# Stage 1 of layer 0 by single k tiles, 1/rms broadcast from a column, and some low parts of weights made by an adding DMA

## The chip, the cores and the metric

The kernel runs on one core of a Trainium2 chip. The metric is the device time of one execution in microseconds (us). Each kernel is run several times; the median counts. A profiled execution gives the trace that the views below are taken from. TensorE is called PE, VectorE DVE, ScalarE ACT, GpSimd POOL and SyncE SP.

## The reference

Two layers of a mixer over 256 latent tokens and 256 context tokens of 2048 features. Cut to what matters here:

```python
for l in range(2):
    shift, scale, gate = split(silu(c) @ w_mod[l] + b_mod[l], 3)   # and the same of c_ctx for the context
    h = rmsnorm(x, g_pre[l]) * (1 + scale) + shift                 # and h_c of ctx
    proj = h @ w_in[l]                                             # 5120 columns: a_u a_v a_g q k v b_g c_x c_g
    y_a = gelu(a_u) * (w_sgu @ rmsnorm(gelu(a_v)) + b_sgu) * silu(a_g)
    y_b = windowed_attention(q, k, v, k_ctx, v_ctx, sink) * silu(b_g)
    y_c = (real(fft2(c_x)) @ w_fourier + b_fourier) * silu(c_g)
    y = rmsnorm(concat(y_a, y_b, y_c) @ w_out[l], g_post[l])
    x = x + gate * y                                               # and ctx in layer 0
```

All is float32. The output is x of the latents after layer 1.

## The kernel before, in words

**Products.** Activations lie feature-major: 16 k tiles of 128 features by 512 tokens (latents, then context). A float32 product is made of three float32r products, `mm3` (L383 to L386): every operand is split into a high part (a cast by ACT) and a low part (the difference, by DVE), and high x high, high x low and low x high are added in PSUM.

**Weights.** The class `Stream` (L329 to L379) hands out `w_in` and `w_out` in halves of 128 x 1024 (512 KB). `emit` loads one into one of three `raw` tiles, lets ACT cast it (`whi`, L367) and DVE subtract (`wlo`, L368); there are four tiles of each. `next` hands out the next half and first emits as many as `NEAR` or `AHEAD = 3` says, so a half is begun when PE comes to the one three before. `pace` then lets a few steps of the other modulation columns follow on DVE (`mod_dve`, L196 to L218).

**Order.** PE's instructions are in the order of the program (`manual_schedule`, L989); the other engines are ordered by the planner, which goes by priority. Work that comes back to PE after other engines had their part stands in generators of the class `Later`; a number given with `yield` is the PE time that shall pass before the next part.

**Start and stage 1 of layer 0.** `ct`, `vecs` and the first constants are loaded, then the 16 tiles of x (L997); ACT squares them and DVE adds the squares (L464 to L468). `col_sums` sums over features on PE, `rstd_cols` (L410) makes 1/rms in a column per 128 tokens with a power on POOL, `rstd_diag` (L417) multiplies the identity by each column on DVE, and `bcast` (L431) multiplies ones by these diagonals, so that 1/rms stands on all partitions. Scale and shift of layer 0 come from PE: `mod_start(k0, nk)` (L154 to L194) loads the columns of `w_mod` of one or two k tiles in four groups of four rows of blocks, each 1 MB for a pair and 512 KB for a single k tile, multiplies them by silu(c) in four column groups of the array (L172), transposes the result on DVE (L177), and adds the four quadrants by four small products (`ps_modc`, L182). Then DVE and ACT make h of the k tile (`make_h`, L445). The first eight k tiles go as pairs, the last eight singly (`PAIRS`, `ALONE`, L24). For each block the loop of `layer` (L524) makes h, does the modulation products of the next block around its own products, and adds to four PSUM tiles of a_v and two of a_u (`start_av`, `start_au`), with k outermost. The heads 2 and 3 of a_u are units of their own behind it (`tunit`, L473, 48 products each).

**PSUM** has eight banks: six `mm` and two `ms` (small results: modulation, sums, broadcasts, transposes).

**Behind stage 1.** Branch A (L580 to L603) applies Gelu on ACT to a_u and a_v, squares, normalises, and multiplies by `w_sgu` on PE (`ps_mix`, L596) 12 units of PE time later; the Fourier branch, gates and attention follow, then the output projection, whose `boundary` (L908) makes x of layer 1 and its 1/rms by the same diagonals.

Of the kernel before, what the change touches and what calls it, by code (L numbers as in the profile page):

```python
# [23 lines left out]
PAIRS, ALONE = [0, 2, 4, 6], list(range(8, KT))  # L24
# [3 lines left out]
def units():  # L28
    """(name, first column, columns, first k tile, k tiles): blocks of w_in of 128 x 2048 each."""
    u = []  # L30
    u += [("av", COL["av"], 512, 4 * i, 4) for i in range(4)]
    u += [("au01", COL["au"], 256, 8 * i, 8) for i in range(2)]
    u += [(f"au{h}", COL["au"] + 128 * h, 128, 0, 16) for h in (2, 3)]
    u += [(f"cx{h}", COL["cx"] + 128 * h, 128, 0, 16) for h in range(4)]
    u += [(f"ag{h}", COL["ag"] + 128 * h, 128, 0, 16) for h in range(4)]
    u += [(f"cg{h}", COL["cg"] + 128 * h, 128, 0, 16) for h in range(4)]
    u += [(f"k{h}", COL["k"] + 128 * h, 128, 0, 16) for h in range(2)]
    u += [("v", COL["v"], 256, 8 * i, 8) for i in range(2)]
    u += [(f"q{h}", COL["q"] + 128 * h, 128, 0, 16) for h in range(8)]
    u += [(f"bg{h}", COL["bg"] + 128 * h, 128, 0, 16) for h in range(8)]  # L40
    return u
# [25 lines left out]
def trunk_kernel(ctx: ExitStack, tc: tile.TileContext, xT, xhalf, cT, wss, wsl, wmod, win, wout0, wout1, const, vec, rows,  # L67
# [24 lines left out]
    # ---- constants  # L92
    ct = sb([P, KT, 2], F32, "ct")
    DMA.dma_start(ct, cT)
    vecs = sb([P, 2, NVEC], F32, "vecs")
    DMA.dma_start(vecs, vec)
# [8 lines left out]
    A.activation(cs, ct, AF.Silu)  # L105
    cpad = sb([P, KT, 32], F32, "kt0")
    V.memset(cpad, 0.0)
    V.tensor_copy(cpad[:, :, 0:2], cs)

    class low:  # L110
        """instructions that may wait for the next `n`."""
# [22 lines left out]
    # ---- modulation: columns [128, 16, stream] of scale, shift and gate  # L134
# [5 lines left out]
    def mod_cols(l, cb, ps8):  # L140
        """ps8 [128, 4, 2]: silu(c) @ w_mod for 512 columns of column block cb."""
        what, j0 = cb // 4, (cb % 4) * 4
        b = vc(l, "bmod")[:, cb * 4:cb * 4 + 4].unsqueeze(2).to_broadcast([P, 4, 2])
        sl = slice(j0, j0 + 4)
        if what == 0:
            V.tensor_tensor(out=sh[l][:, sl], in0=ps8, in1=b, op=ALU.add)
        else:
            dst = (gs[l] if what == 1 else gg0)[:, sl]
            g = vc(l, "gpre" if what == 1 else "gpost")[:, sl].unsqueeze(2).to_broadcast([P, 4, 2])
            V.scalar_tensor_tensor(out=dst, in0=ps8, scalar=1.0 if what == 1 else 0.0, in1=b,  # L150
                                   op0=ALU.add, op1=ALU.add)
            V.tensor_tensor(out=dst, in0=dst, in1=g, op=ALU.mult)

    def mod_start(k0, nk):  # L154
        """scale and shift of k tiles k0 .. k0 + nk - 1 of layer 0 on the tensor engine: yields after
        each unit's products, and before the columns."""
        ps = ms_ps("mod")
        n = 2 * P * nk
        for kg in range(4):
            src = wss[PAIRS.index(k0), kg] if nk == 2 else wsl[ALONE.index(k0), kg]  # L160
            if nk == 1:
                tags = (("mraw", "mraw", "macc", "vv"), ("mg", "mgl", "yo0 yo1", "yo2 yo3"))[k0 % 2][kg]
# [33 lines left out]
    def mod_dve(l, cb, red):  # L196
        """red [128, 2, 16]: sums over the 32 partitions of each quadrant, transposed."""
# [38 lines left out]
    def mod_gate1():  # L236
        """products of silu(c) and the gate's columns of w_mod in layer 1, still to be summed over partitions."""
# [16 lines left out]
    def gate1():  # L254
        """(sum + b_mod) * g_post of layer 1's gate, on all partitions."""
# [23 lines left out]
    NEAR = [1] * 6 + [0] * 6 + [1, 2, 3]  # L279
    LOWC = 60  # L280
    YT = 2.0
# [5 lines left out]
    def pace():  # L287
        """steps of the modulation due per half of a unit, behind the latest weights on the vector engine."""
# [6 lines left out]
    # ---- work of other engines that hands products back to the tensor engine later  # L295
    class Later:
# [19 lines left out]
        def flush(self):  # L316
# [8 lines left out]
            (("yo8 yo9", 1), ("yo10 yo11", 1)), (("yo12 yo13", 1), ("yo14 yo15", 1))]  # L325
    BACK = 8

    # ---- weights: raw -> exact parts hi + lo, in halves of a unit, ahead of their use
    class Stream:  # L329
        AHEAD = 3  # L330

        def __init__(self):
            self.src, self.out, self.pos, self.stop = [], [], 0, 0
            self.place, self.behind = {}, {}
            for l in range(2):
                def half(name, i, h):
                    return win[l, UIDX[name][i], h]
                for i in range(2):
                    self.src += [half("av", 2 * i, 0), half("au01", i, 0), half("av", 2 * i, 1),
                                 half("av", 2 * i + 1, 0), half("au01", i, 1), half("av", 2 * i + 1, 1)]  # L340
                for i, u in enumerate(UNITS):
                    if u[0] not in ("av", "au01"):
# [5 lines left out]
                if l == 0:  # L348
                    n = len(self.src) - 2 * HELD
                    self.place[n] = (("mraw", 2), ("mraw", 2))  # L350
                    self.place[n + 1] = (("macc", 1), ("mg", 1))
            for i, tags in enumerate(TAIL):
                self.place[len(self.src) - len(TAIL) + i] = tags

        def emit(self):
            tags = self.place.get(len(self.out), (("whi", NHI), ("wlo", NLO)))
            r = sb([P, 1024], F32, "raw", NRAW)
            DMA.dma_start(r, self.src[len(self.out)])
            hi, lo = ([sb([P, 1024 // len(t[0].split())], F32R, tag, t[1]) for tag in t[0].split()] for t in tags)
            with ExitStack() as after:  # L360
# [27 lines left out]
    def part(w, c):  # L388
        """columns c of both parts; a part is a tile or a list of tiles side by side."""
# [19 lines left out]
    # ---- per-token reciprocal rms from sums over features  # L409
# [7 lines left out]
    def rstd_diag(sums, n, dim):  # L417
        r = rstd_cols(sums, n, dim)
        dg = w2k([P, n, P])
        for j in range(n):  # L420
            V.tensor_scalar(out=dg[:, j], in0=ident, scalar1=r[:, j:j + 1], scalar2=None, op0=ALU.mult)
# [9 lines left out]
    def bcast(dg, n):  # L431
        ps = ms_ps("rb")
        PE.matmul(ps[:, 0:n * P], ones, dg.rearrange("p a b -> p (a b)"), start=True, stop=True)
        return ps

    # ---- streams in feature-major tiles
    yo = [None] * KT
# [7 lines left out]
    def make_h(l, k, rb, streams):  # L445
        """h = x * rstd * gs + sh, as hi + lo; rb: rstd over the tokens of `streams`."""
# [26 lines left out]
    def tunit(n, sl=None):  # L473
        """feature-major product of one unit of 128 columns: PSUM [128, n]."""
# [18 lines left out]
    blocks = [(k, 2) for k in PAIRS] + [(k, 1) for k in ALONE]  # L493

    # ---- one layer, up to the inputs of the output projection
    def layer(l):
# [12 lines left out]
        # a_v (token-major) and two heads of a_u, k outermost  # L509
        av = [mm_ps("av") for _ in range(nt)]  # L510
        au = [mm_ps("au") for _ in range(2)]
# [12 lines left out]
        for i, (k0, nk) in enumerate(blocks):  # L524
            mod = mod_start(*blocks[i + 1]) if l == 0 and i + 1 < len(blocks) else iter(())

            def step():
                next(mod, None)

            for k in range(k0, k0 + nk):  # L530
                made = prep_h(l, k)
            if l == 1 and i == 0:
# [7 lines left out]
            for _ in range(2 if nk == 2 else 4):  # L540
                step()
            start_av(k0, range(nt))
            if nk == 2:
                start_au(k0)
                step()
                step()
                start_av(k0 + 1, range(nt // 2))
            step()
            if nk == 2:
                start_av(k0 + 1, range(nt // 2, nt))  # L550
# [28 lines left out]
        # branch A  # L579
        def branch_a():  # L580
            vt = [w2k([P, 512]) for _ in range(nt)]
            ss = sb([P, 4], F32, "ss")
            for j in range(2):
# [8 lines left out]
            yield 12.0 if l == 0 else 7.0  # L592
            for h in range(4):
# [9 lines left out]
                yield (12.0 if h == 1 else 2.0) if l == 0 else (7.0 if h == 1 else 2.0)  # L603

        # branch C
# [137 lines left out]
        for h in (2, 3):  # L743
# [56 lines left out]
    # ---- output projection  # L800
# [107 lines left out]
    def boundary(s, acc):  # L908
        """x1 = x0 + gate * y / rms(y) of stream s in place, and its own 1 / rms."""
# [11 lines left out]
        dg = rstd_diag(ps[:, 0:2], 2, D)  # L921
# [31 lines left out]
        dg = rstd_diag(ps[:, 0:2], 2, D)  # L953
# [5 lines left out]

    def prep_h(l, k):  # L960
        new_h(k)
        if l == 0:
            return make_h(0, k, rb0, [0, 1])
        return make_h(1, k, rbs[0], [0])
# [24 lines left out]
    with tc.manual_schedule(engines={mybir.EngineType.PE}):  # L989
# [3 lines left out]
        A.copy(identr, raw[:, 0:P])  # L993
        A.copy(cst[:, 0:NFIRST - P], raw[:, P:])
        for k in range(KT):
            yo[k] = sb([P, T], F32, f"yo{k}")
            DMA.dma_start(yo[k], xT[k])  # L997
# [3 lines left out]
        m = mod_start(*blocks[0])  # L1001
# [8 lines left out]
        next(m)  # L1010
        W.emit()
        W.emit()
        list(m)
# [81 lines left out]
```

## Time and profile before

| | us |
|---|---|
| median of 3 runs | 1170.88 (1170.09 to 1171.65) |
| span of the profiled execution | 1167.9 |
| PE waits for its first operand | 17.0 |
| first product of a_v starts | 37.3 |
| last product of a_u's first two heads starts | 136.4 |
| POOL busy in all | 17.3 |

The profiled execution's own time is its span, from the first to the last instruction; what lies around it in a timed run is not in the profile. In the timeline a row has start, duration, engine, line, operation, output and inputs and the number merged; a float32 product has two records. The durations of PE overlap, since products are pipelined: the distance of two starts tells what one costs, not its duration. In the stretches the columns are busy time of each engine with its number of instructions, the granted clock of PE (1.00 is full), the share of the DMA engines and GB/s.

### The profile page before, as it was taken

What the parts mean: (1) busy time and instruction counts of PE and PEld (TensorE: products, weight loads), DVE (VectorE), ACT (ScalarE), POOL (GpSimd) and SP (SyncE); (2) the same over time, 40 slices, a digit from 0 to 9 for tenths busy, and PEclk for the clock granted to TensorE, in tenths of its full rate; (3) what the DMA queues carried; (4) which work ended last, traced back from release to release, by engine and by line L of the source; (5) the groups of instructions that cost most, each with busy time, mean ns of one, the idle gap of its engine ahead of it and who ended that gap; (6) DMA issues with size and microseconds to landing.
All of it is one profiled execution on the core that took longest, in us unless ns stands there. A gap on an engine that the chain in (4) does not pass through costs nothing.

```text
span 1167.9 us, 17483 instructions
## 1 busy us (share of the span) xinstructions
PE 1136.0 (97%) x6656; PEld 953.7 (82%) x6656; DVE 881.8 (76%) x1469; ACT 509.8 (44%) x914; POOL 17.3 (1%) x23
## 2 busy tenths in 40 slices
PE   3999999999999999999999999999999999999996
PEld 1466688888898888888888888889899999997885
DVE  5454498888988878798989886495896678888554
ACT  4222513322224667632533233365563278745442
POOL 0000000000000000000000000200000000000001
PEclk9999999999999999999999999999999999999998
DMA  9999765466665334455466665365656665688563
GB/s 339 378 387 357 254 196 166 145 202 193 200 200 178 105 114 136 134 175 173 158 199 209 205 216 162 109 207 173 205 158 205 203 200 178 195 269 244 190 187 120
DMA packets 73892, 234.32 MB, mean 201 GB/s; under 512 B 8528, under 2 KB 9680, under 8 KB 73808
## 3 DMA queue, kind: packets, MB, share of 16 engines
q1 hardware_dynamic: 73808, 233.21, 61.6%
q8 instruction: 52, 0.85, 0.3%
q14 instruction: 32, 0.26, 0.1%
HBM read 231.08 MB, written 2.10 MB: 200 GB/s over the span
## 4 chain that ended last, share of the span: by engine, by line
PE 92%; DVE 3%; DMA 2%; ACT 2%; issue 1%; POOL 0%; SPq 0%; DVEq 0%; ACTq 0%; POOLq 0%
PE ps_t L384 20%; PE ps_t L385 20%; PE ps_t L386 20%; PE ps_mod L172 3%; PE ps_av L384 2%; PE ps_y L386 2%; PE ps_y L384 2%; PE ps_y L385 2%; PE ps_av L385 2%; PE ps_av L386 2%; PE ps_v L386 1%; PE ps_v L384 1%; PE ps_v L385 1%; PE ps_tp L722 1%; PE ps_au L384 1%
## 5 line engine op out<-in xcount | busy, mean ns | idle before, releaser
L384 PE MATMUL ps_t<-hh,whi 128*128 128x512 f32 (+1 forms) x1296 | 452.1, 349 | 0.0
L386 PE MATMUL ps_t<-hh,wlo 128*128 128x512 f32 (+1 forms) x1296 | 447.4, 345 | 0.0
L385 PE MATMUL ps_t<-hl,whi 128*128 128x512 f32 (+1 forms) x1296 | 447.0, 345 | 0.0
L367 ACT CAST whi<-raw 128x1024 fp32r<-128x1024 f32 x218 | 228.2, 1050 | 397.3 <-PE ps_t L385 274.4
L368 DVE TENSOR_TENSOR wlo<-raw,whi 128x1024 fp32r<-128x1024 f32 x218 | 265.3, 1220 | 99.1 <-ACT whi L367 98.8
L384 PEld LDWEIGHTS ps_t<-hh,whi 128*128 128x128 f32 x1296 | 244.9, 189 | 34.3 <-issue 4.6
L386 PEld LDWEIGHTS ps_t<-hh,wlo 128*128 128x128 f32 x1296 | 244.7, 189 | 30.6
L385 PEld LDWEIGHTS ps_t<-hl,whi 128*128 128x128 f32 x1296 | 244.9, 189 | 28.9 <-issue 0.5
L209 DVE SCALAR_TENSOR_TENSOR macc<-mraw,cs,macc 128x512 f32<-128x512 f32 x360 | 249.9, 745 | 17.6 <-DMA mraw<-in_wmod_dram 17.5
L455 ACT ACTIVATE hh<-w2k,sh 128x256 fp32r<-128x256 f32 x64 | 29.0, 502 | 61.4 <-DVE w2k L451 61.4
L384 PE MATMUL ps_y<-whi,hh 128*128 128x512 f32 x112 | 45.0, 401 | 0.0
L386 PE MATMUL ps_y<-whi,hl 128*128 128x512 f32 x112 | 43.8, 392 | 0.0
L385 PE MATMUL ps_y<-wlo,hh 128*128 128x512 f32 x112 | 43.7, 390 | 0.0
L384 PE MATMUL ps_av<-whi,hh 128*128 128x512 f32 x96 | 40.0, 416 | 0.0
L385 PE MATMUL ps_av<-wlo,hh 128*128 128x512 f32 x96 | 37.9, 395 | 0.4 <-DVE wlo L368 0.4
L172 PE MATMUL ps_mod<-hh,kt 128*32 128x512 f32 x64 | 21.5, 649 | 17.0 <-DMA hh<-in_wss_dram 17.0
L386 PE MATMUL ps_av<-whi,hl 128*128 128x512 f32 x96 | 37.6, 392 | 0.0
L386 PE MATMUL ps_v<-whi,hl 128*128 128x256 f32 x128 | 36.2, 283 | 0.0
L384 PE MATMUL ps_v<-whi,hh 128*128 128x256 f32 x128 | 36.2, 283 | 0.0
L385 PE MATMUL ps_v<-wlo,hh 128*128 128x256 f32 x128 | 36.2, 283 | 0.0
L468 DVE TENSOR_TENSOR acc<-acc,w2k 128x512 f32<-128x512 f32 (+1 forms) x33 | 21.2, 641 | 18.7 <-ACT w2k L467 17.2
L401 ACT CAST w2k<-ps_tp 128x512 fp32r<-128x512 f32 x40 | 23.5, 587 | 22.8 <-PE ps_scc L385 12.0
(292 smaller groups left out, 1491.8 us busy)
## 6 DMA issues: line engine op xcount, KB each, us to landing
raw<-in_win_dram SPq DMA_DIRECT2D x160, 512.0 KB, 4.1
mraw<-in_wmod_dram SPq DMA_DIRECT2D x128, 512.0 KB, 4.3
raw<-in_wout_dram SPq DMA_DIRECT2D x64, 512.0 KB, 4.2
hh<-in_wss_dram SPq DMA_DIRECT2D x32, 256.0 KB, 5.6
hl<-in_wss_dram SPq DMA_DIRECT2D x32, 256.0 KB, 5.4
yo<-in_xT_dram SPq DMA_DIRECT2D x16, 256.0 KB, 5.4
mraw<-in_wsl_dram SPq DMA_DIRECT2D x8, 512.0 KB, 6.9
yo<-in_wsl_dram SPq DMA_DIRECT2D x16, 256.0 KB, 7.2
```

The lines of the kernel that those rows point to most:

```text
L172: PE.matmul(ps[32 * kk:32 * kk + 32, 0:n], cpad[:, kg * 4 + kk], ws[kk], start=kg == 0, stop=kg == 3, tile_position=(0, 32 * kk))
L209: V.scalar_tensor_tensor(out=acc[:, s], in0=w[:, kk % 2], scalar=c, in1=acc[:, s], op0=ALU.mult, op1=ALU.add)
L367: A.copy(ph, r[:, c])
L368: self.last = V.tensor_tensor(out=pl, in0=r[:, c], in1=ph.bitcast(F32), op=ALU.subtract)
L384: PE.matmul(ps, st[0], mv[0], start=start, stop=False)
L385: PE.matmul(ps, st[0], mv[1], start=False, stop=False)
L386: PE.matmul(ps, st[1], mv[0], start=False, stop=stop)
L401: A.copy(hi, src)
L455: first = A.activation(hh[k][:, sl], t[:, sl], AF.Identity, bias=sh[l][:, k, s:s + 1])
L468: V.tensor_tensor(out=acc[:, sl], in0=acc[:, sl], in1=q[:, sl], op=ALU.add)
L722: PE.transpose(tp[:, (2 * j + b) * P:(2 * j + b + 1) * P], src, ident)
```

## The change

- Layer 0's stage 1 goes by single k tiles throughout. Ahead of a_v of k tile k all products of the modulation of k + 1 stand. A third head of a_u is added in the same loop, in one of the two `ms` banks; its unit behind the loop goes. Two steps of other modulation are put at each of the last two k tiles.
- DVE, ACT and SP are ordered by hand too until the last k tile but one; `LOADS` and `SPLITS` say at which k tile a half of weights is loaded and split. x is loaded ahead of the constants and `vecs`.
- 48 products of ones by ones stand on PE ahead of the first modulation.
- `bcast` takes the column of 1/rms itself, spread over 128 columns, as the stationary operand and the identity as the moving one; `rstd_diag` goes, also in the boundaries.
- In layer 0, every other half of weights from the 22nd on (42 halves) gets its low part otherwise: ACT writes the negated high part, and a DMA issued by POOL adds the raw weights to it.
- Branch A's delays are 9 and 4 instead of 12 and 12 in layer 0.

```diff
-PAIRS, ALONE = [0, 2, 4, 6], list(range(8, KT))
+PAIRS, ALONE = [0], list(range(KT))
...
-    NEAR = [1] * 6 + [0] * 6 + [1, 2, 3]
+    NEAR = [0] * 14 + [1, 2, 3]
+    LOADS = [0, 1, 2, 4, 5, 6, 6, 8, 9, 10, 12, 13, 14]
+    SPLITS = [1, 2, 3, 5, 6, 7, 7, 9, 10, 11, 13, 14, 15]
+    WARM = 48
+    AU2 = [(("hh12 hl12", 1), ("hh13 hl13", 1)), (("yo4 yo5", 1), ("yo6 yo7", 1))]
...
+                    self.by_dma |= set(range(22, n, 2))
...
+            if tags == (("whi", NHI), ("wlo", NLO)) and len(self.out) in self.by_dma:
+                A.copy(hi[0], r)
+                A.activation(lo[0], hi[0].bitcast(F32), AF.Copy, scale=-1.0)
+                G.dma_start(lo[0], r, accum_op=ALU.add)
+                self.out.append((hi, lo))
+                return
...
-    def rstd_diag(sums, n, dim):
-        r = rstd_cols(sums, n, dim)
-        dg = w2k([P, n, P])
-        for j in range(n):
-            V.tensor_scalar(out=dg[:, j], in0=ident, scalar1=r[:, j:j + 1], scalar2=None, op0=ALU.mult)
-        return dg
-    def bcast(dg, n):
+    def bcast(r, n):
         ps = ms_ps("rb")
-        PE.matmul(ps[:, 0:n * P], ones, dg.rearrange("p a b -> p (a b)"), start=True, stop=True)
+        for j in range(n):
+            PE.matmul(ps[:, j * P:(j + 1) * P], r[:, j:j + 1].to_broadcast([P, P]), ident, start=True, stop=True)
         return ps
...
+        au = [mm_ps("au") for _ in range(2)] + [ms_ps("au") for _ in range(1 - l)]
...
+            if l == 0:
+                mm3(au[2], part(au2w, slice((k % 8) * P, (k % 8 + 1) * P)), (hh[k], hl[k]), k == 0, k == KT - 1)
...
+        if l == 0:
+            for k in range(KT):
+                new_h(k)
+                make_h(0, k, rb0, [0, 1])
+                m = mod_start(k + 1, 1) if k + 1 < KT else iter([None] * 4)
+                for _ in range(4):
+                    next(m)
+                for _ in range(LOADS.count(k)):
+                    W.load()
+                for _ in range(SPLITS.count(k)):
+                    W.emit()
...
+                start_av(k, range(nt))
+                list(m)
+                if k == KT - 2:
+                    first_stage.close()
...
+                start_au(k)
...
-            yield 12.0 if l == 0 else 7.0
+            yield 9.0 if l == 0 else 7.0
...
+        first_stage.enter_context(tc.manual_schedule(engines={EN.DVE, EN.Activation, EN.SP}))
+        DMA.dma_start(ct, cT)
+        for k in range(KT):
+            DMA.dma_start(yo[k], xT[k])
...
+        W.load()
+        ps = ms_ps("ones")
+        for _ in range(WARM):
+            PE.matmul(ps[:, 0:P], ones, ones, start=True, stop=True)
+        m = mod_start(0, 1)
+        next(m)
         ps = ms_ps("rs")
         col_sums(ps, acc0, 4)
-        dg = rstd_diag(ps[:, 0:4], 4, D)
+        r0 = rstd_cols(ps[:, 0:4], 4, D)
+        W.emit()
         next(m)
-        rb = bcast(dg, 4)
+        next(m)
+        next(m)
+        rb = bcast(r0, 4)
         rb0 = w2k([P, T])
         V.tensor_copy(rb0, rb)
+        W.load()
+        W.load()
+        list(m)
         W.emit()
         W.emit()
-        list(m)
         layer(0)
```

More of the change, by code (lines that the diff above doesn't have):

```diff
@@ L90, in ms_ps @@
         return psum.tile([P, 512], F32, tag="ms", bufs=2, name=f"ps_{name}_{cnt[0]}")
+    yo = [sb([P, T], F32, f"yo{k}") for k in range(KT)]
     ct = sb([P, KT, 2], F32, "ct")
-    DMA.dma_start(ct, cT)
     vecs = sb([P, 2, NVEC], F32, "vecs")
-    DMA.dma_start(vecs, vec)
     cst = sb([P, NKEEP - P], F32, "cst")
@@ L161, in mod_start @@
             if nk == 1:
-                tags = (("mraw", "mraw", "macc", "vv"), ("mg", "mgl", "yo0 yo1", "yo2 yo3"))[k0 % 2][kg]
+                odd = ("hh14 hl14", "hh15 hl15") if k0 < 8 else ("yo0 yo1", "yo2 yo3")
+                tags = (("mraw", "mraw", "macc", "vv"), ("mg", "mgl") + odd)[k0 % 2][kg]
             else:
@@ L333, in __init__ @@
             self.src, self.out, self.pos, self.stop = [], [], 0, 0
-            self.place, self.behind = {}, {}
+            self.raws = []
+            self.place, self.behind, self.by_dma = {}, {}, set()
             for l in range(2):
@@ L338, in __init__ @@
                 for i in range(2):
-                    self.src += [half("av", 2 * i, 0), half("au01", i, 0), half("av", 2 * i, 1),
+                    third = [half("au2", 0, i)] if l == 0 else []
+                    if l == 0:
+                        self.place[len(self.src) + 2] = AU2[i]
+                    self.src += [half("av", 2 * i, 0), half("au01", i, 0), *third, half("av", 2 * i, 1),
                                  half("av", 2 * i + 1, 0), half("au01", i, 1), half("av", 2 * i + 1, 1)]
                 for i, u in enumerate(UNITS):
-                    if u[0] not in ("av", "au01"):
+                    if u[0] not in ("av", "au01") + ("au2",) * (l == 0):
                         self.src += [win[l, i, 0], win[l, i, 1]]
@@ L491, in hold_unit @@
         return ps
-    blocks = [(k, 2) for k in PAIRS] + [(k, 1) for k in ALONE]
+    blocks = [(k, 2) for k in range(0, 8, 2)] + [(k, 1) for k in range(8, KT)]
     def layer(l):
@@ L521, in start_au @@
                 mm3(au[j][:, 0:n], part(auw, c), (hh[k][:, 0:n], hl[k][:, 0:n]), k == 0, k == KT - 1)
+            if l == 0:
+                mm3(au[2], part(au2w, slice((k % 8) * P, (k % 8 + 1) * P)), (hh[k], hl[k]), k == 0, k == KT - 1)
             later.tick(PASS * 512 * nt + PASS * n * 2)
[L524 to L528, printed above, removed]
+        if l == 0:
+            for k in range(KT):
[8 more added lines that the diff above has]
+                    W.emit()
+                if k % 2 == 0:
+                    avw = W.next()
+                if k % 4 == 0:
+                    auw = W.next()
+                if k % 8 == 0:
+                    au2w = W.next()
+                start_av(k, range(nt))
+                list(m)
+                if k == KT - 2:
+                    first_stage.close()
+                if k >= KT - 2:
+                    for _ in range(2):
+                        with low(LAG), tc.issue_after(W.last.ins):
+                            next(mods)
+                start_au(k)
+        for i, (k0, nk) in enumerate(blocks if l else ()):
             for k in range(k0, k0 + nk):
-                made = prep_h(l, k)
-            if l == 1 and i == 0:
+                new_h(k)
+                made = make_h(1, k, rbs[0], [0])
+            if i == 0:
                 W.behind = {len(W.out): made, len(W.out) + 1: made}
@@ L539, in layer @@
                 auw = W.next()
-            for _ in range(2 if nk == 2 else 4):
-                step()
             start_av(k0, range(nt))
@@ L544, in layer @@
                 start_au(k0)
[L545 to L550, printed above, removed]
+                start_av(k0 + 1, range(nt))
             start_au(k0 + nk - 1)
@@ L582, in branch_a @@
             ss = sb([P, 4], F32, "ss")
-            for j in range(2):
+            for j in range(len(au)):
                 A.activation(ytmp(j), au[j][:, 0:n], AF.Gelu_apprx_tanh)
@@ L742, in layer @@
         state["phase"] = f"au{l}"
-        for h in (2, 3):
+        for h in range(len(au), 4):
             ps = tunit(n)
@@ L920, in boundary @@
         col_sums(ps, acc[:, sl], 2)
-        dg = rstd_diag(ps[:, 0:2], 2, D)
+        dg = rstd_cols(ps[:, 0:2], 2, D)
         yield 2.2
@@ L958, in boundary @@
         rbs[s] = r
[L960 to L964, printed above, removed]
     def after_start(l):
@@ L987, in boundary_ctx @@
                 yield YH
-    with tc.manual_schedule(engines={mybir.EngineType.PE}):
+    EN = mybir.EngineType
+    first_stage = ExitStack()
+    with tc.manual_schedule(engines={EN.PE}):
+        first_stage.enter_context(tc.manual_schedule(engines={EN.DVE, EN.Activation, EN.SP}))
+        DMA.dma_start(ct, cT)
+        for k in range(KT):
+            DMA.dma_start(yo[k], xT[k])
         raw = w2k([P, NFIRST])
         DMA.dma_start(raw, const[:, 0:NFIRST])
[L993 to L997, printed above, removed]
+        DMA.dma_start(vecs, vec)
+        A.activation(cs, ct, AF.Silu)
+        V.tensor_copy(cpad[:, :, 0:2], cs)
         acc0 = sb([P, T], F32, "acc")
@@ L1000, in trunk_kernel @@
             add_sq(acc0, yo[k], FULL, k == 0)
-        m = mod_start(*blocks[0])
+        A.copy(identr, raw[:, 0:P])
+        A.copy(cst[:, 0:NFIRST - P], raw[:, P:])
+        W.load()
[3 more added lines that the diff above has]
+        m = mod_start(0, 1)
         next(m)
```

18 lines of the change are left out of this document (9 added, 9 removed).

## The prediction

> **What bounds the kernel now.** I read first the page's busy row and its row of waits on TensorE, to see whether any engine but PE can set the end.
>
> ```profile
> PE 1136.0 (97%) x6656; PEld 953.7 (82%) x6656; DVE 881.8 (76%) x1469; ACT 509.8 (44%) x914; POOL 17.3 (1%) x23
> ```
>
> The waits of PE, longest first, are these:
>
> ```profile
> PE ps_mod L172 <- DMA hh<-in_wss_dram: 17.0, 1, 17.0
> PE ps_o L385 <- DVE w2k L402: 1.7, 3, 1.0
> PE ps_rb L433 <- DVE w2k L421: 1.4, 1, 1.4
> PE ps_modc L182 <- DVE w2k L177: 0.9, 1, 0.9
> ```
>
> So PE waits 17 us for its first operand and about 6 us in all the rest. A busy PE is not a dense one, so I looked at the starts in the timeline of PE: the 128x512 products of `mm3` start 0.23 us apart from the first product of a_v to the last stage, and only seven gaps over 0.6 us are left behind 37 us (0.6 to 1.3 us each; six of them in layer 1). What can be won is therefore ahead of the first product of a_v, or PE work itself. The start:
>
> ```profile
> 17.02 1.03 PE L172 MATMUL ps_mod<-hh,kt 128*32 128x512 f32 x1 [17.02 <-DMA hh<-in_wss_dram]
> ...
> 36.33 1.04 PE L172 MATMUL ps_mod<-hl,kt 128*32 128x512 f32 x2
> 37.30 0.50 PE L384 MATMUL ps_av<-whi,hh 128*128 128x512 f32 x1
> ```
>
> From 17 to 37 us PE handles modulation weights as they land. That this is the DMA's pace shows in the timeline of SP, which issues one 256 KB piece for each that lands (385 GB/s; the stretches of 10 us have 390, 396 and 386 GB/s from 10 to 40 us):
>
> ```profile
> 11.46 0.33 SPq L169 DMA_DIRECT2D hh<-in_wss_dram  x1
> 12.14 0.33 SPq L169 DMA_DIRECT2D hl<-in_wss_dram  x1
> 12.82 0.33 SPq L169 DMA_DIRECT2D hh<-in_wss_dram  x1
> ```
>
> **0.68 us a piece.** Count of the pieces that must land ahead of the first a_v: x 16, the pair's block 16, three halves of weights 6, half of the next pair 8: 46. The first x is used at 6.02 us (timeline of ACT), so the last lands at 6.0 + 45 x 0.68 = 36.6; the trace has 36.3 to 36.7. The model holds.
>
> **The start after.** x is issued ahead of `vecs` and `const`, as second instruction of SP instead of fourth: 0.94 us earlier (2.12 to 1.18), first x at 5.1. Ahead of a_v of k = 0 PE now has all products of k tiles 0 and 1: x 16, the first half of weights 2, k tile 0 8, two halves 4, k tile 1 8, and the moved constants 0.7: 38.7 pieces. 5.1 + 37.7 x 0.68 = 30.7; plus the 1.0 us from landing to a_v that before shows: **31.7 instead of 37.3, 5.6 us earlier.** The other chain to a_v: x complete at 15.3, its sums by DVE at about 18.2 (0.79 us per add as now), rows' sums and 1/rms 22, 1/rms broadcast after the products of k tile 0 (land 22.6) at 24.2, copy 0.69, columns 0.5, two splits that DVE now has in between by hand (1.22 + 2 x 0.69), h 2.1: 30.9. It is hidden by 0.8 us. The diagonals (4 x 283 ns and the 1.4 us wait) go, but lie on this covered chain: nothing. The products of ones: 48 of 128x128 at 0.22 us (transposes L722: two records 0.109 us apart), twice that at half clock, end between 11.5 and 22 us; at 22 the chain ends near 32.3 and a_v is 0.6 us later. I take nothing, bound 0.6.
>
> **Stage 1 after.** A period of a single k tile in before:
>
> ```profile
> 94.74 0.50 PE L384 MATMUL ps_av<-whi,hh 128*128 128x512 f32 x1
> ...
> 97.71 0.25 PE L182 MATMUL ps_modc<-w2k,cst 128*32 128x4 f32 x8
> 97.89 0.50 PE L384 MATMUL ps_au<-hh,whi 128*128 128x512 f32 x1
> ...
> 99.46 0.64 PE L172 MATMUL ps_mod<-mg,kt 128*32 128x256 f32 x8
> ...
> 101.33 0.50 PE L384 MATMUL ps_av<-whi,hh 128*128 128x512 f32 x1
> ```
>
> 6.59 us: 2.97 for a_v and its end, 0.18 columns, 1.57 for six products of a_u, 1.87 modulation. Three more products of the third head: 0.69, so 7.28. From the first a_v: 14 x 7.28, then 5.3 (k = 14, no modulation) and 5.0 (k = 15): **112.2 us**, end at 143.9. Before goes from 37.3 to 136.6, 99.3 us, and then does the third head as a unit of its own, 48 products, 11.1 us: 110.4. So after does 1.8 us more in this part (one more k tile's products are left at the first a_v, four more column steps; against 1.4 us that PE stands for DMA in the first two pairs now). **5.6 - 1.8 = 3.8 us won**, if nothing holds PE. What could: the DMA needs 8 pieces and on average 1.75 of weights per k tile, 9.75 x 0.68 = 6.6 us against 7.28, so PE stays the bound; SP's buffers are two k tiles deep. DVE in order by hand per k tile: transpose 0.45, a split 1.22, columns 0.5, h 1.8, and columns come 3.2 us into the period, h about 6: 1.3 us of slack. The third head keeps one of the two `ms` banks, so the next modulation must wait until DVE has read the columns, 0.6 us into the 2.1 us of a_u: hidden, 1 to 1.5 us per k tile if a late split were ahead.
>
> **Clock.** The stretches of 10 us show the granted clock at 0.83 from 20 to 30 us: PE had only short products and waits there, and the broadcast (L433, 1.13 us a record against 0.59 for the same shape at L611) ran at half speed. After, k tile 1's products are 0.43 us of PE per 1.36 us of DMA just ahead of a_v, where before's 512-wide ones fill the time. So half clock at the first a_v is about as likely as not; it costs half of up to 3.4 us of dense work. I take **0.7**, bound 0 to 1.7. The Trainium skill, TensorE: Matmul & The Clock Gate (The HAM clock gate), says that the clock halves after an idle window of about 3.4 us and returns after a busy one; the products of ones would then warm PE at 5 us and be lost again while it waits for k tile 0. By that rule the sum would have the whole 1.7.
>
> **Behind stage 1.** Branch A's first products (L596) come at 151.7 in before, 15.1 us behind a_u's end, and their operand was ready at 147.0 (DVE L591), 4.7 us ahead. With one unit less and the delay 9 instead of 12 they come 42 products and the 1.9 us of `ps_mg` behind: 11.8 us. The operand: ACT has one more Gelu (0.6) and one more cast (1.05) ahead, and begins about 1 us earlier with a_v: 11.0 us, 0.8 us of slack. I take nothing, bound 1.5.
>
> **Low parts by the adding DMA.** 42 of 218 subtractions (1.22 us, L368) leave DVE: 51 us. PE never waited for them in layer 0, so nothing is won. They become an ACT negation and a POOL DMA. Lead: a half is begun when PE starts the half three before, 3 x 5.5 = 16.5 us ahead. Cost: cast 1.05, negation 1.05 (the cast's row), issue at most 1.0 (POOL's L414), transfer: no adding DMA is in the trace; a 512 KB load lands in 4.1 us (row of issues), twice that if its destination is read too. 11.4 us at most, 5 us hidden; from below, nothing. I take nothing. ACT's extra 42 x 1.05 us: it waits 1.3 to 2 us before each head's exponentials, which the negation fills:
>
> ```profile
> 404.29 0.30 ACT L687 ACTIVATE es<-nm,skb 128x4 f32<-128x4 f32 x1 [1.27 <-DVE nm L684]
> ```
>
> The queue on POOL holds nothing PE needs until the boundary. The transfers cost DMA time where it is busiest:
>
> ```profile
> 500.00:600.00 100.00, 100.00 (x464) 82.67 (x463) 90.28 (x136) 36.19 (x52) 0.00 (x0) 1.00 0.56 178
> 600.00:700.00 100.00, 100.00 (x441) 82.45 (x440) 89.24 (x127) 29.97 (x45) 0.00 (x0) 1.00 0.66 210
> ```
>
> One per unit of 11 us: at twice a plain 512 KB (1.36 us) 0.25 of the engines, 0.8 to 0.9 in all. The diagonals of the boundaries (8 x 283 ns of DVE) have no PE wait behind them: nothing.
>
> **Sum.** Against the profiled execution: 1167.9 - 3.8 + 0.7 = 1164.8 of span. The runs' median of 1170.88 is 3.0 above the span; I keep that: **1167.8**.
>
> **Rivals.** *Half clock and branch A take the gain* (22%): the clock's whole 1.7 and the late products' 1.5 leave 0.6: 1170.3. For it: both are within a microsecond of happening. *More is won* (12%): the clock stays full and the early DMA waits go too, 1166. *DMA becomes stage 1's bound* (8%), slower: it decides from 0.747 us a piece (351 GB/s); at the lowest stretch of stage 1, 327 GB/s from 80 to 90 us, a k tile takes 9.75 x 0.80 = 7.8, 0.5 x 14 = 7 us lost: 1174. Against it: 383 to 403 GB/s while the queue was full. *The adding DMA fills the DMA engines* (10%), slower: loads and modulation then come late in the gates and the output projection, DVE stands in order, and PE follows. It decides at (1 - 0.61) x 11 = 4.3 us of all 16 engines each, three times a plain transfer; at four times 1.1 us for each of some 18 units: 20 us less the gain, 1188. The Trainium skill, DMA: Bandwidth & Descriptors (Anatomy of one DMA), gives 2.0 us plus bytes by 436 GB/s for a POOL-issued DMA, an estimate of 3.2 us here, inside my bounds; no run shows it for an adding one.
>
> **How the numbers follow.** Forecast 48%, 1166.8 to 1169.3. What this measurement can tell from no change is 0.2%, 2.3 us: 1168.5. Faster: three quarters of the forecast and the 12%: 0.48. Slower: the last two: 0.19 with a little of the second rival. Range 1165 to 1175: it leaves out the adding DMA's case and a few points at the low end.
>
> **What would show it.** First a_v near 31.7 and 7.3 us per k tile; end of stage 1 near 144; granted clock in 27 to 35 us; the wait of ps_mix; no PE wait on wlo between 160 and 640 us; DMA share under 0.9 there. Wrong if x lands no earlier, if PE waits for columns each k tile, or if adding transfers take over 13 us from cast to landing.

## The result and the profile after

| | before | after |
|---|---|---|
| median of the runs, us | 1171.09 | 1196.88 (1194.26 to 1200.35) |
| ratio, 95% interval | | 1.0222 [1.0202, 1.0241] |
| span of the profiled execution, us | 1167.9 | 1198.6 |
| first product of a_v, us | 37.3 | 31.67 |

The forecast was 1167.8, within 1165 to 1175. The kernel became 2.2% slower; the time lies outside the range, 9 us beyond the slowest rival of the prediction (1188). (The profiled execution of after took 1200.35, the longest of its four runs, some 3 us above their median. Everything below that is read from traces comes from one execution of each kernel; that of e10 lies 9 us above its median, that of e7 4 us below, so a few us between two kernels there say little.)

The page of after, its row of busy time, its row of the POOL queue, and the two rows of the chain that ended last:

```profile
PE 1158.4 (97%) x6926; PEld 980.3 (82%) x6926; DVE 833.5 (70%) x1433; ACT 550.9 (46%) x958; POOL 57.2 (5%) x65
...
q0 software_dynamic: 6048, 22.02, 10.3%
...
PE 62%; DMA 16%; DVE 16%; ACT 3%; issue 2%; SPq 0%; POOL 0%; DVEq 0%; ACTq 0%; POOLq 0%
```

PE is as "busy" as before (97%) and DVE has less to do (70% instead of 76%), and yet the chain goes over DMA and DVE for a third of the span. The busy share says nothing here; the chain does. The start came as forecast (timeline of PE, start, duration, engine, line):

```profile
1.06 13.79 PE L1035 MATMUL ps_ones<-ones 128*128 128x128 f32 x96 [1.06 <-DVE ones L98]
18.68 1.08 PE L170 MATMUL ps_mod<-mraw,kt 128*32 128x256 f32 x8 [3.83 <-DMA mraw<-in_wsl_dram]
...
31.67 0.50 PE L403 MATMUL ps_av<-whi,hh 128*128 128x512 f32 x1
```

So the loss lies behind it. To place it I matched the first product of each unit of 48 products (`ps_t`) in both traces and took the difference, after minus before. Three of the experiments below stand beside it.

| time in before, us | 188 | 230 | 377 | 493 | 575 | 652 | 718 | last product |
|---|---|---|---|---|---|---|---|---|
| what runs | Fourier | gates | queries | gates | projection | projection | its end | layer 1 |
| after | -4.6 | 1.7 | 7.4 | 8.4 | 8.1 | 8.2 | 31.0 | 30.7 |
| e1, no adding DMA | -4.6 | -3.9 | -4.3 | -4.8 | -5.1 | -5.4 | -5.2 | -3.8 |
| e7, fewer steps | -4.9 | 2.6 | 2.1 | 14.7 | 16.6 | 22.3 | 22.4 | 21.9 |
| e9, third tile | -4.7 | -4.7 | -5.2 | -1.4 | -1.7 | -2.0 | 1.6 | 4.3 |

After is 4.6 us early at 188 us, then loses some 6 us up to the gates, 6 more up to the queries, and 23 us in the output projection. Layer 1, which has no adding DMA, keeps the difference. The waits of PE in after, longest first:

```profile
PE ps_t L405 <- DVE wlo L387: 7.7, 4, 3.4
PE ps_t L405 <- DMA wlo<-raw: 7.1, 1, 7.1
PE ps_mod L170 <- DMA mraw<-in_wsl_dram: 3.8, 1, 3.8
PE ps_sc L403 <- ACT w2k L420: 3.7, 1, 3.7
```

Only half of what PE waits for in low parts is made by the DMA (7.1 us, one wait at the projection's end). The other half (7.7 us, four waits, all in the projection) is made by *DVE*: halves whose making the change did not touch are late as well.

The waits are not the whole loss. From 188 us to the projection's end they add up to 22 us, where after loses 36 against before. Most of the rest is the clock: behind the waits the granted clock falls to 0.50, in five stretches (218.6 to 222.0, 375.6 to 379.0, 669.1 to 672.6, 710.1 to 713.5 and 730.6 to 740.8 us), and there the 128x512 products start 0.43 us apart instead of 0.23. PE works for some 20 us of these stretches, so half speed costs about 10 us, 6 to 7 of them in the projection. Before has no such stretch between 28 and 1161 us. One row of after, with the mean clock of 0.84:

```profile
700.00:740.00 40.00, 29.45 (x110) 23.10 (x110) 22.92 (x31) 13.18 (x19) 1.74 (x2) 0.84 0.61 182
```

DVE's largest waits tell what it stands for, first in before, then in after (L209 and L207 of before are L207 and L205 of after):

```profile
DVE macc L209 <- DMA mraw<-in_wmod_dram: 17.5, 17, 2.4
...
DVE macc L207 <- DMA mraw<-in_wmod_dram: 2.4, 3, 1.1
```

```profile
DVE macc L207 <- DMA mraw<-in_wmod_dram: 65.0, 36, 5.1
DVE macc L205 <- DMA mraw<-in_wmod_dram: 30.4, 11, 7.2
```

DVE waits nearly five times as long for the weights of the *modulation*. It works in order, and the next half's subtraction stands behind. The chain of waits of after shows it in the output projection (start, duration, what):

```profile
682.41 6.06 DMA mraw<-in_wmod_dram
...
688.56 1.81 DVE macc L207 x3
...
690.55 0.76 DVE macc L207
...
691.33 6.24 DMA mraw<-in_wmod_dram
...
697.66 2.75 DVE macc L207 x4
...
700.43 0.76 DVE macc L207
...
701.21 4.52 DMA mraw<-in_wmod_dram
```

A tile of `mraw` lands, DVE multiplies it, the tile is free, SP loads it again: 8.9 us, then 9.9 us. There are two such tiles. At 2.8 steps per unit of 10.94 us (before's 13 units from 575.4 to 717.6 us) each tile may take 2 / 2.8 x 10.94 = **7.8 us** from load to load, and a little less on average, since every eighth step also passes its result through one of the tiles (`t` in `mod_dve`). The rows of DMA issues between 600 and 720 us (number, size, median us to landing) say why it takes longer; before, then after:

```profile
mraw<-in_wmod_dram SPq DMA_DIRECT2D x23, 512.0 KB, 4.0
```

```profile
mraw<-in_wmod_dram SPq DMA_DIRECT2D x23, 512.0 KB, 5.8
raw<-in_wout_dram SPq DMA_DIRECT2D x18, 512.0 KB, 5.8
wlo<-raw POOLq DMA_DIRECT2D x9, 512.0 KB, 6.8
```

A landing took 4.0 us and takes 5.8. From the issue of its load to the end of its fourth product a tile was in use for 7.9 us in before and is for 9.1 in after (median of the loads issued from 575 to 720 us). In both DVE begins 0.09 us behind the landing in the median, so a tile's time is landing and products, and no waiting for DVE. Before had thus no slack either: DVE already stood there for `mraw`. Its waits from 600 to 720 us, before, then after:

```profile
DVE macc L209 <- DMA mraw<-in_wmod_dram: 10.2, 9, 2.4
...
DVE macc L207 <- DMA mraw<-in_wmod_dram: 0.4, 1, 0.4
```

```profile
DVE macc L207 <- DMA mraw<-in_wmod_dram: 30.7, 16, 5.1
DVE macc L205 <- DMA mraw<-in_wmod_dram: 5.1, 3, 3.3
```

PE felt nothing of the 10.6 us and feels the 35.8. That fits the 16.5 us by which a half is begun ahead of PE (the prediction's lead), and it fits that after loses nothing yet in the projection's first 75 us; no run varies this lead.

### The profile page after: what moved, and what is told of

Same layout as the page of the kernel before. It is cut to its first block, busy times and chain, and to the rows that moved or that the text cites. A ratio compares the mean times of both kernels' runs of the same rounds, so it can differ in the third digit from the quotient of the medians.

```text
span 1198.6 us, 18071 instructions
## 1 busy us (share of the span) xinstructions
PE 1158.4 (97%) x6926; PEld 980.3 (82%) x6926; DVE 833.5 (70%) x1433; ACT 550.9 (46%) x958; POOL 57.2 (5%) x65
## 3 DMA queue, kind: packets, MB, share of 16 engines
q1 hardware_dynamic: 70352, 233.21, 58.3%
q0 software_dynamic: 6048, 22.02, 10.3%
## 4 chain that ended last, share of the span: by engine, by line
PE 62%; DMA 16%; DVE 16%; ACT 3%; issue 2%; SPq 0%; POOL 0%; DVEq 0%; ACTq 0%; POOLq 0%
DMA mraw<-in_wmod_dram 13%; PE ps_t L403 11%; PE ps_t L405 11%; PE ps_t L404 11%; DVE macc L207 8%; PE ps_mod L170 3%; DVE wlo L387 2%; PE ps_av L403 2%; PE ps_y L403 2%; PE ps_y L405 2%; PE ps_y L404 2%; PE ps_av L404 2%; PE ps_av L405 2%; PE ps_au L403 1%; PE ps_au L405 1%
## 5 line engine op out<-in xcount | busy, mean ns | idle before, releaser
L405 PE MATMUL ps_t<-hh,wlo 128*128 128x512 f32 (+1 forms) x1280 | 444.5, 347 | 14.9 <-DVE wlo L387 7.7
L386 ACT CAST whi<-raw 128x1024 fp32r<-128x1024 f32 x174 | 181.4, 1047 | 274.3 <-PE ps_t L404 105.9
L207 DVE SCALAR_TENSOR_TENSOR macc<-mraw,cs,macc 128x512 f32<-128x512 f32 x360 | 249.9, 746 | 65.4 <-DMA mraw<-in_wmod_dram 65.0
L387 DVE TENSOR_TENSOR wlo<-raw,whi 128x1024 fp32r<-128x1024 f32 x174 | 211.6, 1219 | 84.7 <-ACT whi L386 84.4
L374 ACT CAST whi<-raw 128x1024 fp32r<-128x1024 f32 x42 | 44.1, 1051 | 69.9 <-PE ps_t L404 56.9
L376 POOL DMA_DIRECT2D wlo<-raw x42 | 36.8, 876 | 538.7 <-ACT wlo L375 496.5
L375 ACT ACTIVATE wlo<-whi 128x1024 fp32r<-128x1024 f32 x42 | 44.6, 1062 | 1.1
```

Source lines behind the costliest of these rows:

```text
L207: V.scalar_tensor_tensor(out=acc[:, s], in0=w[:, kk % 2], scalar=c, in1=acc[:, s], op0=ALU.mult, op1=ALU.add)
L374: A.copy(hi[0], r)
L375: A.activation(lo[0], hi[0].bitcast(F32), AF.Copy, scale=-1.0)
L376: G.dma_start(lo[0], r, accum_op=ALU.add)
L386: A.copy(ph, r[:, c])
L387: self.last = V.tensor_tensor(out=pl, in0=r[:, c], in1=ph.bitcast(F32), op=ALU.subtract)
```

## The experiments

The theories that the expectations name: the load that the adding transfers put on the DMA engines (L); the raw tile held until the transfer is done (H); modulation steps bunched, since `W.last` is set by DVE's subtractions only and half of these are gone (B); and, formed when H and B had fallen, Q: the landings lengthen, two tiles of `mraw` no longer carry 2.8 steps per unit, and DVE, in order, makes the other low parts late. The projection's loss is the growth of the lag from 575 to 718 us (23 us in after).

**e1_no_adding_dma**: the adding DMA is taken out, the rest of the change kept.

```diff
-                    self.by_dma |= set(range(22, n, 2))
```

> All low parts by DVE again; the rest of the change stays. The changed kernel's trace wins 4.5 us by the third unit behind stage 1 (its units start 4.5 us ahead of those of before) and loses 35 us later in layer 0. If all of the loss is the adding DMA's: 1171.1 - 4.5 = 1166.6 us, no PE wait over 1 us in layer 0. Rival, the loss comes from the new order of DVE, ACT and SP or from branch A's shorter delays: over 1180.

1167.59 us (before beside it 1171.54), ratio 0.9968 [0.9956, 0.998]. All the loss is the adding DMA's, 29.3 us; the rest of the change wins 4 us.

**e2_add_from_hbm** and **e3_anchor**: the first takes the addend from the weights in memory (against H), the second puts a copy of one column on DVE, which sets `W.last` (against B).

```diff
-                G.dma_start(lo[0], r, accum_op=ALU.add)
+                G.dma_start(lo[0], self.src[len(self.out)], accum_op=ALU.add)
```

```diff
+                self.last = V.tensor_copy(anchor, hi[0].bitcast(F32)[:, 0:1])
                 G.dma_start(lo[0], r, accum_op=ALU.add)
```

> The adding DMA reads the weights from HBM a second time instead of from the raw tile, so the raw tile is free once ACT has cast it. Theory H (the raw tile is held until the adding DMA has landed, SP stands in order at the next raw load and the modulation loads behind it come late): at most 1172. Theory L (the adding transfers take time of the DMA engines, every modulation load lands later, DVE stands at it with the low parts behind): no better than the changed kernel, 1190 to 1205. Theory B (modulation steps stand in bunches of three behind every other low part, since the adding path leaves no DVE instruction to put them behind): also 1190 to 1200.

> The adding DMA stays, but each half that it serves leaves a one-column copy on DVE that the next modulation steps are put behind, so the steps alternate as in before. Theory B: at most 1175. Theories H and L: 1188 to 1200.

1197.02, 1.0214 [1.018, 1.0249], and 1197.36, 1.0221 [1.0172, 1.027]: neither H alone nor B alone. The projection loses 15.4 and 20.2 us. (e2's addend comes from memory, a second read of the weights; its transfers took the same 25.0% of the engines from 580 to 720 us as after's.)

**e4_load_alone**: DVE makes all low parts as before; POOL adds two blocks of 480 columns of the high part into a spare tile nobody reads, at the same halves. The bytes (20.65 MB against 22.02) and the share of the engines (10.4% against 10.3%) are those of after.

```diff
+                for i in (0, 480):
+                    G.dma_start(spare, hi[0][:, i:i + 480].bitcast(F32), accum_op=ALU.add)
```

> DVE makes all low parts, and POOL issues adding DMAs of 94% of the bytes from the high part into a spare tile that nobody reads. The DMA engines carry nearly the same load; no raw tile is held and no step bunched. Computes the same output, the added transfers are waste. Theory L: 1185 or more. Theories H and B: at most 1170.

1179.88, 1.0077 [1.0059, 1.0094], between what the expectation gave for L and for H and B: 12.3 of the 29.3 us without any low part being late by DMA, 3.3 us of it in the projection. The landing of `mraw` there is 5.0 us (580 to 720 us) and a tile is in use for 8.0 us.

**e5_both_freed**: e2's and e3's edits together.

> Both single remedies at once: the adding DMA takes its second operand from the weights in memory, so the raw tile is free after ACT's cast, and a one-element copy on DVE per half spreads the modulation steps as before. Theory HB (the 17 us beyond the load come from holding raw or from bunched steps, either being enough alone): near e4's 1180. Theory Q (the load makes every landing in the output projection longer, and the two modulation buffers, DVE in order and the late low part do the rest whatever frees raw): 1190 to 1197 again, 13 to 23 us of it lost between 660 and 748 us.

1195.49, 1.0206 [1.0183, 1.0229], 20 us lost in the projection. H and B fall together too, as what makes the projection's loss. Its chain of waits in the projection is again landing, products, landing.

**e6_projection_only**: `range(80, n, 2)`, so that only the projection's 13 halves are made by the DMA.

> Only the last 13 of the 42 halves, those of the output projection, get their low part by the adding DMA; the 29 before stay on DVE. If the projection's loss is made there (theory Q and HB alike): 1167.6 plus about 20 = 1187, and the lag against the kernel before stays at -5 us until 660 us. If the loss is made of the same price per transfer everywhere: 1167.6 + 29.3 x 13 / 42 = 1177. If it needs the 8 us that the kernel is late by then, or steps put off earlier: under 1172.

1186.86, 1.013 [1.0111, 1.0149]. The lag stays at -4 us until 652 us and is 16.1 at 718. So 13 transfers cost 20 us where the modulation runs at 2.8 steps, and the other 29, at 1.8 to 2.2 steps, the remaining 10: the price is the stage's, not the transfer's.

**e7_fewer_steps**: the modulation's rate is moved from the projection to the query units.

```diff
-    RATE = dict(... q0=1.8, bg0=2.2, out0=2.8,
+    RATE = dict(... q0=3.4, bg0=2.2, out0=2.0,
```

> All 42 adding DMAs, but the modulation runs 2.0 instead of 2.8 steps per unit in the output projection, and 3.4 instead of 1.8 in the query units, so that all steps are still done. Theory Q: a step's buffer is in use for its landing 5.7 us, its four products 2.7 us and the issue 0.4 us, 8.8 us in all; two buffers at 2.8 steps in 11 us allow 7.9, at 2.0 steps 11.0. So the projection's loss falls from 23 us to under 6; the query units, where the DMA share is 0.54, may give some of it back: 1176 to 1188. If the low part's or the raw tile's own lateness makes the loss: 23 us lost again between 660 and 748, 1195 or more.

1197.9, 1.0225 [1.0185, 1.0265]. In the projection Q holds: 5.8 us lost instead of 23, nearly all of it in the first unit. Its last load of `mraw` is issued at 659 us; from 652 to 718 us, with the adding DMAs running and hardly any modulation beside them, only 0.1 is lost, so the low part's own way alone costs PE nothing there. In the stretches of 40 us (us, then busy time of PE, PEld, DVE, ACT, POOL, granted clock, DMA share, GB/s) PE is whole:

```profile
640.00:680.00 40.00, 40.00 (x178) 33.11 (x177) 29.35 (x41) 16.05 (x24) 3.49 (x4) 1.00 0.79 224
680.00:720.00 40.00, 40.00 (x184) 32.84 (x183) 8.09 (x12) 17.95 (x25) 3.49 (x4) 1.00 0.57 155
```

But I had expected 1176 to 1188, and the query units lose 12.6 us instead (377 to 493 us). The eight query units take 124 us in before, 15.5 each, since the attention's products stand between; at 3.4 steps a tile has 2 / 3.4 x 15.5 = 9.1 us, and was in use for 9.8 (median, 377 to 493 us). In before, at 1.8 steps, a landed tile lay there 5.9 us until DVE came to it; in e7 0.6. The loss goes where the steps go; the expectation failed by not putting its own formula to the query units.

**e8_load_and_hold**: e4 with the raw tile as source.

```diff
-                    G.dma_start(spare, hi[0][:, i:i + 480].bitcast(F32), accum_op=ALU.add)
+                    G.dma_start(spare, r[:, i:i + 480], accum_op=ALU.add)
```

> As e4 (DVE makes all low parts, POOL adds two blocks of 480 columns into a spare tile), but from the raw tile instead of the high part: the raw tile stays in use until both transfers are done. The load is the same, the low part isn't late and the modulation steps are spread. If holding raw under load makes the projection's loss: 1190 or more, 15 us and more of it between 660 and 748 us. If it doesn't: e4's 1180 within 3 us, and the low part's own way by ACT, POOL and DMA is what is left.

1194.18, 1.0184 [1.016, 1.0208]. The total is what was expected if holding mattered under load, the place isn't: the projection loses 6.6 us, while the lag grows by 16 us from 352 to 377 us (7.1 in e4; 5.4 in after), where PE waits once 13.9 us for the attention's `ps_sc` (and the clock is halved behind it). Holding raw under load can cost as much; e5, where it isn't held, shows that it isn't what costs in after's projection.

**e9_third_buffer** and **e10_six_small_tiles**: all 42 adding DMAs and the old rate, three tiles of `mraw` instead of two; the space is taken from the small tiles (`W2K` 6 instead of 7), and e10 has only that. (e9 also puts a few small sums of layer 1 into tiles that others use.)

```diff
-    W2K = 7
+    W2K = 6
...
-                    w = sb([P, 2, 512], F32, "mraw", 2)
+                    w = sb([P, 2, 512], F32, "mraw", 3)
```

> The changed kernel with all 42 adding DMAs and the old rate of 2.8 steps, but three tiles instead of two for the modulation's loads; the space is taken from the small-result tiles, six instead of seven. Theory Q (two tiles in flight, each in use for landing, products and issue, 8.8 to 10.5 us, are the bound): three tiles allow 11.8 us per step, so the projection loses under 5 us instead of 23 and the whole is 1172 to 1182. If the bound is a rate (the DMA engines' or DVE's time) and not the number of tiles: 15 us or more lost between 660 and 748 us, 1190 or more.

> Control for e9: the changed kernel with six small-result tiles instead of seven, two tiles for the modulation's loads. Both theories: within 4 us of the changed kernel's 1197.

e9: **1172.43**, 1.0014 [1.0, 1.0028]. e10: 1194.61, 1.0212 [1.0168, 1.0255]. Against its control the third tile gives back 22.2 us, and the projection loses 3.3 instead of 19.6. The DMA rows of e9 between 600 and 720 us:

```profile
raw<-in_wout_dram SPq DMA_DIRECT2D x23, 512.0 KB, 5.3
mraw<-in_wmod_dram SPq DMA_DIRECT2D x20, 512.0 KB, 5.8
wlo<-raw POOLq DMA_DIRECT2D x9, 512.0 KB, 8.0
```

The landings are no shorter than in after (5.8 again; the adding transfer even 8.0 instead of 6.8), and the engines are busier: after first, then e9.

```profile
640.00:680.00 40.00, 37.99 (x159) 30.58 (x158) 27.90 (x41) 12.81 (x18) 2.61 (x3) 0.96 0.75 225
```

```profile
640.00:680.00 40.00, 39.72 (x173) 32.03 (x172) 36.04 (x53) 13.05 (x18) 2.61 (x3) 1.00 0.89 277
```

At a DMA share of 0.89 PE runs almost without a gap, at 0.75 it waited. So it was not the engines' capacity but the number of loads in flight: each step took as long, and a third one was under way. In e9 a landed tile lies 0.8 us in the median before DVE comes to it (0.09 in after), and DVE's waits for `mraw` from 600 to 720 us are 11.8 us instead of 35.8.

All kernels with two tiles and 2.8 steps: how long a tile is in use (loads issued from 575 to 720 us), how long DVE waits for `mraw` (580 to 720 us), and the projection's loss.

| | e1 | before | e4 | e8 | e5 | e3 | e6 | e2 | e10 | after |
|---|---|---|---|---|---|---|---|---|---|---|
| tile in use, median us | 7.3 | 7.9 | 8.0 | 8.5 | 8.5 | 8.6 | 8.6 | 8.8 | 8.9 | 9.1 |
| DVE waits for `mraw`, us | 5.2 | 12.4 | 15.8 | 20.0 | 29.5 | 35.8 | 37.1 | 29.7 | 36.3 | 35.8 |
| projection's loss, us | -0.1 | - | 3.3 | 6.6 | 20.0 | 20.2 | 20.0 | 15.4 | 19.6 | 22.9 |

The longer a tile is in use and the longer DVE waits for it, the more is lost. The size does not follow the tile's time alone (e8 against e5): where the low part goes over ACT, POOL and the DMA, a late `raw` costs more, as in the 6.8 us that PE's last wait in after's projection spends on the adding transfer itself.

**e11_no_add_no_ones**: e1 with `WARM = 0`.

> As e1 (no adding DMA), without the 48 products of ones. The granted clock is halved before the first a_v in any case, since PE waits from 14.9 to 18.7 us and works little until 31: the first a_v stays at 31.7 within 0.7 us and the whole within 1.5 us of e1's 1167.6. If the products of ones win what they are put there for, the first a_v comes over 1 us later and the clock returns later than 31 us.

**1165.24**, 0.9947 [0.9932, 0.9962], the fastest version run; it beats both kernels. a_v starts at 30.94 instead of e1's 31.63, and the whole is 2.4 us shorter than e1, both just outside what was expected. By 230 us the two have the same lag (-3.8 and -3.9); they part in layer 1 (-5.4 and -3.8 at the last product), where e1 waits 4.9 us and e11 3.0 for `ps_x`. The intervals of e1 and e11, which were not timed side by side, overlap. The products of ones win nothing; whether leaving them out wins, these runs don't settle.

## Why the prediction was wrong, point by point

- **The start: right.** First a_v 31.7 predicted, 31.67 measured; 7.28 us per k tile, 7.25 measured; the stage's end 143.9, and 143.4 measured. DMA did not become the bound of stage 1. (Two slips that decided nothing: the terms listed for the covered chain add up to 30.1 us, not 30.9, unless the broadcast's own time is counted, and the 383 to 403 GB/s leave out the stretch from 50 to 60 us with 366.)
- **The clock: 0.7 us too much.** The granted clock is full from 7.0 to 17.2 us, half until 30.85, and full again just before a_v. The products of ones end at 14.9 us, so the clock fell 2.4 us behind them. The Trainium skill's rule (TensorE: Matmul & The Clock Gate, The HAM clock gate) agrees in that the warmth of the ones is lost during the wait; but the modulation's own products brought the clock back 0.8 us ahead of a_v, so the sum had none of the rule's 1.7.
- **Branch A: right**, no wait of `ps_mix`.
- **Everything but the adding DMA: right together.** e1 measured 1167.59, where the forecast, which set the adding DMA at nothing, said 1167.8. Beside its own before e1 wins 4.0 us; the forecast had 3.1, or 3.8 without the 0.7 for the clock.
- **"Low parts by the adding DMA ... I take nothing": this step failed**, by 29.3 us. Its own numbers held: cast 1.05, negation 1.06, issue 0.88 and landing 6.9 make 9.9 us, inside the 11.4 (whose terms add up to 11.3), and far from the 13 that I had named as what would prove me wrong. What it left out is what the transfers do to *other* loads. I had covered only the path from the cast to PE, 16.5 us of lead. The modulation's path had no slack: in before's projection its two tiles were in use for 7.9 us where 7.8 were allowed, DVE already waited 10.6 us for them, and then each landing grew by 1.8 us. DVE's waits became 35.8 us, its own low parts came late, and PE's waits brought the half clock with them. The profile of before held the 10.6 us. The path that I had covered did cost something too, at one place: the projection's last adding transfer, begun late, made PE wait 7.1 us.
- **The rival "fills the DMA engines": right place, wrong condition.** I had loads and modulation late in the gates and the projection, DVE in order, PE behind, and 1188. But I let it decide at 4.3 us of all engines per transfer, and gave it 10%. The queue's row gives 10.3% of 1198.6 us for 42 transfers, 2.9 us each (a plain 512 KB took 1.6: 58.3% for the 445 of SP's queue). By my condition nothing should have happened, and e9 shows that at that load little need happen (1172.43, and 0.84 to 0.89 of the engines from 600 to 680 us, the 0.8 to 0.9 that I had worked out): landing time and tiles in flight decided, before the engines were full. The Trainium skill's figure for a POOL-issued DMA (DMA: Bandwidth & Descriptors, Anatomy of one DMA), from which I had estimated 3.2 us, does not hold here: beside the other loads the adding transfer landed in 6.9 us.
- **"51 us leave DVE, nothing is won"**: DVE's busy time fell by 48 us and its waits for `mraw` rose by over 75.

What stays open: why the same bytes lengthen landings less in e4 (5.0 us) than in after (5.7, both 580 to 720 us); what makes up the 5 us between e9 and e1; and how much of after's 12 us between 188 and 377 us goes by the same cycle: e9 has none of it, but e4 and e8, whose low parts are all made by DVE, lose 7 and 16 us at the attention's wait, and no run isolates why.

## What to carry to other kernels

Before adding transfers beside a stream that is fed through n tiles, work out that stream's slack: n tiles divided by the steps per unit of time, less landing, work and issue of one step. A DMA share under 1 does not protect it: here landings grew by 1.8 us while the share went from 0.65 to 0.75. Where the engine that takes the loads already waits for them, as DVE did, there is no slack, even if the bounding engine feels nothing. And follow every engine that takes such loads in order: what stands behind them is late as well, though nothing about it was changed.

## What the runs showed of the hardware

- A 512 KB transfer with addition from one on-chip tile to another cost 2.9 us of all 16 DMA engines, 1.9 times a plain load, 0.88 us of POOL for its issue, and landed in 6.9 us in the median. In the projection the plain loads of 512 KB beside it landed in 5.8 us instead of 4.0.
- In after a wait of PE of 1.3 us (up to 217.4 us), in a stretch of otherwise dense products, was followed by a granted clock of 0.50 from 218.6 to 222.0 us; one of 1.9 us (up to 668.1 us) by 0.50 from 669.1 to 672.6. At half speed 3.4 us of products are 1.7 us lost, on top of the wait.
- In e11, with no products ahead, the granted clock reads 1.00 in every stretch up to 150 us (the trace holds no record of the clock ahead of 30.6 us), and yet the modulation's products (128x256) run at 1.08 us a row until 29 us and at 0.64 from 29 on. With the ones ahead (after) the clock reads 0.50 in that stretch. After first, then e11:

```profile
20.00:30.00 10.00, 9.44 (x72) 5.78 (x73) 4.98 (x10) 2.18 (x3) 1.95 (x1) 0.50 1.03 402
```

```profile
20.00:30.00 10.00, 9.44 (x75) 6.07 (x77) 5.13 (x11) 2.18 (x3) 1.95 (x1) 1.00 1.03 404
```

PE's busy time is the same 9.44 us in both: a granted clock of 1.00 ahead of the first record does not say that PE ran at full speed.
